# Down projection of a hybrid encoder step: the last token group ends bank by bank, and the first rows' operands are split before the up projection's last sums

## Chip, cores and metric

The kernel runs on one core of a Trainium2 chip. The metric is device time in microseconds (us) of one execution; below, times without a unit are us. Before the change, three runs took 1442.82, 1444.15 and 1447.29; the median is 1444.15.

## The reference

One inference step of a one-layer encoder over 1024 prompt tokens and 32 sample tokens of width 1024: a mixer of three kinds of heads, then a convolutional feed-forward block. Only the latter matters here:

```python
def conv_ffn(xn, buf, w_up, conv_w, conv_b, w_down):
    up = xn @ w_up
    up, buf = causal_dwconv(up, buf, conv_w, conv_b)
    gate, val = jnp.split(up, 2, axis=-1)
    return (jax.nn.gelu(gate, approximate=True) * val) @ w_down, buf
...
h, ffn_buf = conv_ffn(rms_norm(x, g_ffn_pre[l]), ...)
x = x + rms_norm(h, g_ffn_post[l])
```

`w_up` is 1024 x 5632 and `w_down` 2816 x 1024, all float32. The convolution runs over the last three tokens. The inner width of 2816 makes 22 rows of 128 channels, called rows 0 to 21 here.

## The kernel before

**Precision.** A float32 product is made of three matmuls. `split` (line 104) makes a high part by a cast on ScalarE (line 106) and a low part by a subtraction on VectorE (line 109); `mm3` (lines 99 to 102) adds high x high, high x low and low x high in one PSUM bank. So each operand needs a cast and a subtraction before TensorE can use all of it.

**Up projection.** `up_all` (line 1208) goes over the 22 rows; each is done in two blocks of columns (274 and 256), and each block by seven half-size products instead of eight (Strassen-like). `up_block` (line 1150) copies some of the sums out of PSUM on ScalarE (`keep`, line 1159) and adds them on VectorE (line 1164). Its last step, the product p7 with its copy and two sums, is held back and run inside the next block; the very last one stands behind the loop as `next(late, None)`. `up_finish` (line 1190) then moves the tokens' borders on GpSimd, does the convolution of the row's gate and value (one activation on ScalarE and two multiply-adds on VectorE each), the gelu and the product, and stores the h row to DRAM (`h_d`, line 1206).

**Down projection.** `down_all` (line 1239) covers the tokens in three groups of tiles of 128 tokens: tiles 0, 1 and the 32 sample tokens; tiles 2, 3, 4; tiles 5, 6, 7. In each group it goes over all 22 rows again. `load_h` (line 1267) loads the group's columns of an h row into a staging tile `hr` (two buffers), splits it into `hh` and `hl` (two buffers each), loads 128 x 1024 weights into a raw tile (two buffers, shared with the up projection's weights) and splits each half of these with `weight_halves` (line 1117; tag `op`, seven buffers, each of one half's high and low part).

The first group makes the result transposed: eight banks, each of 128 output channels by 288 tokens, 24 matmuls a row. The other two groups make it upright: for each of three token tiles two banks of 512 output channels, 18 matmuls a row. All 22 rows are added in these six banks, so that they are all done only with row 21.

`finish` (line 1248) ends a token tile: squares with a running sum on ScalarE (line 1256), a product with the gain on VectorE (line 1258), three tiny operations on GpSimd for the root of the mean (lines 1260, 218 and 219), and for each half one multiply-add with the residual on VectorE (line 1264) and one store (line 1265). Its statistics tile `fss` has two buffers. The residuals are loaded four rows before the end (`residual`, line 1242).

**What sets the order.** The instructions are written in program order, and a planner, which runs a simulation of the engines' times, orders each engine's queue from it: what is written earlier has the higher priority, and something written later may be drawn forward when its inputs and a free buffer are there and the engine is idle in the simulation. The resulting order on each engine is fixed. All loads and stores are issued from one queue, SyncE's (SPq).

Of the kernel before, what the change touches and what calls it, by code (L numbers as in the profile page):

```python
# [8 lines left out]
F32 = mybir.dt.float32  # L9
F32R = mybir.dt.float32r  # L10
# [9 lines left out]
DEC = 32  # L20
NTOK = SEQ + DEC
DFF = 2816
NF = DFF // 128
# [12 lines left out]
DGROUPS = [(0, 1, 8), (2, 3, 4), (5, 6, 7)]  # L36


def fcol(u):

    return 128 * u if u < 4 else SMP if u == 8 else GAP_P + 2 + 128 * (u - 4)
# [5 lines left out]
            p6=("S2", "T2"), p7=("S3", "T3"))  # L47
# [43 lines left out]
def body(ctx: ExitStack, tc: tile.TileContext, a: dict):  # L91
    nc = tc.nc
    act, dve, pool, pe, sp = nc.scalar, nc.vector, nc.gpsimd, nc.tensor, nc.sync
# [5 lines left out]
    def mm3(ps, lh, rh, first, last, **kw):  # L99
        pe.matmul(ps, lh[0], rh[0], start=first, stop=False, **kw)  # L100
        pe.matmul(ps, lh[0], rh[1], start=False, stop=False, **kw)  # L101
        return pe.matmul(ps, lh[1], rh[0], start=False, stop=last, **kw)  # L102

    def split(hi, lo, src, eng=None, heng=None):
        if heng is None:
            act.copy(hi, src)  # L106
        else:
            heng.tensor_copy(hi, src)
        (eng or pool).tensor_tensor(lo, src, hi.bitcast(F32), op=ALU.subtract)  # L109
# [1004 lines left out]
            res.append(r)  # L1114
        return res

    def weight_halves(name, src):
        t = praw[1].tile([128, 2, 512], F32R, tag="op", name=name, bufs=7)
        split(t[:, 0], t[:, 1], src, dve)
        return t[:, 0], t[:, 1]  # L1120

# [83 lines left out]
        dve.tensor_tensor(ys[0], ys[0], ys[1], op=ALU.mult)  # L1205
        sp.dma_start(h_d[f], ys[0])

    def up_all(pw_, W0, X, uus, py):

        raw, W = {}, {0: W0}  # L1210
        late = None
        for f in range(NF):
            uu = uus[f % len(uus)]
            if f + 1 < NF:
                raw[f + 1] = up_raw(f + 1)
            for s in range(2):
                if s == 1 and f + 1 < NF:
                    ops = up_operands(f + 1, raw.pop(f + 1))
                    W[f + 1] = next(ops)
                    for _ in ops:  # L1220
                        pass
                blk = up_block(pw_, f, s, W[f], X[s], uu)
                next(blk)
                if late:
                    next(late, None)
                    if s == 0:
                        up_finish(py(), f - 1, uus[(f - 1) % len(uus)])
                        W.pop(f - 1)
                next(blk)
                yield  # L1230
                next(blk)
                late = blk
                yield
        next(late, None)
        up_finish(py(), NF - 1, uus[(NF - 1) % len(uus)])

    praw = []

    def down_all(ph, p6, gp):
        xres = {}  # L1240

        def residual(u):
            n = 128 if u < 8 else DEC
            x = p6.tile([128, 1024], F32, tag="xres", name=f"fr{u}", bufs=4)
            sp.dma_start(x[:n], x2_d[128 * u:128 * u + n, :])
            xres[u] = x

        def finish(u, n, src):

            x = xres.pop(u)  # L1250
            ss = p6.tile([128, 4], F32, tag="fss", name=f"gss{u}", bufs=2)
            jk = p6.tile([128, 1024], BF16, tag="fjk", name=f"gjk{u}", bufs=2)
            ys = []
            for hf in range(2):
                c = slice(512 * hf, 512 * hf + 512)
                act.activation(jk[:n, c], src[hf], AF.Square, accum_out=ss[:n, 2 + hf:3 + hf])
                y = p6.tile([128, 512], F32, tag="yt", name=f"yt{u}{hf}", bufs=4)
                dve.tensor_tensor(y[:n], src[hf], gp[:n, c], op=ALU.mult)
                ys.append(y)
            pool.tensor_tensor(ss[:n, 0:1], ss[:n, 2:3], ss[:n, 3:4], op=ALU.add)  # L1260
            rstd_of(ss[:n, 1:2], ss[:n, 0:1], n, 1, 1024)
            for hf in range(2):
                c = slice(512 * hf, 512 * hf + 512)
                dve.scalar_tensor_tensor(x[:n, c], ys[hf][:n], ss[:n, 1:2], x[:n, c], op0=ALU.mult, op1=ALU.add)
                sp.dma_start(a["yp"][128 * u:128 * u + n, c] if u < 8 else a["ys"][:, c], x[:n, c])

        def load_h(g, f, spans, w):
            r = ph.tile([128, 384], F32, tag="hr", name=f"hr{g}_{f}", bufs=2)
            for (c0, c1, o) in spans:
                sp.dma_start(r[:, o:o + c1 - c0], h_d[f, :, c0:c1])  # L1270
            hh = ph.tile([128, 384], F32R, tag="hh", name=f"hh{g}_{f}", bufs=2)
            hl = ph.tile([128, 384], F32R, tag="hl", name=f"hl{g}_{f}", bufs=2)
            split(hh[:, :w], hl[:, :w], r[:, :w], dve)
            wr = praw[0].tile([128, 1024], F32, tag="raw", name=f"wd{g}_{f}r", bufs=2)
            sp.dma_start(wr, a["w_dn"][f])
            return hh, hl, [weight_halves(f"wd{g}_{f}{hf}", wr[:, 512 * hf:512 * hf + 512]) for hf in range(2)]

        def spans_of(us):
            spans, off, w = [], {}, 0
            for u in us:  # L1280
                n = 128 if u < 8 else DEC
                off[u] = w
                if spans and spans[-1][1] == fcol(u):
                    spans[-1][1] += n
                else:
                    spans.append([fcol(u), fcol(u) + n, w])
                w += n
            return spans, off, w

        def banks_of(g, m):  # L1290

            where = [(psf, "xw", 4)] * 4 + [(psb, "big", 3)] * 3 + [(psf, "sx", 1)]
            return [p.tile([128, 512], F32, tag=t, name=f"pd{g}_{i}", bufs=b) for i, (p, t, b) in enumerate(where[:m])]


        us = DGROUPS[0]
        spans, off, w = spans_of(us)
        banks = banks_of(0, 8)
        for f in range(NF):
            hh, hl, wd = load_h(0, f, spans, w)  # L1300
            if f == NF - 4:
                for u in us:
                    residual(u)
            for d in range(8):
                c = slice(128 * (d % 4), 128 * (d % 4) + 128)
                mm3(banks[d][:, :w], [t[:, c] for t in wd[d // 4]], (hh[:, :w], hl[:, :w]), f == 0, f == NF - 1)
        acc = p6.tile([128, 8, 288], F32, name="accd")
        for d in range(8):
            (act.copy if d % 2 else dve.tensor_copy)(acc[:, d, :], banks[d][:, :w])

        def turned(u):
            n = 128 if u < 8 else DEC
            src = []
            for hf in range(2):
                p, t, b = ((psb, "big", 3), (psf, "sx", 1))[hf]
                ps = p.tile([128, 512], F32, tag=t, name=f"pt{u}{hf}", bufs=b)
                for d in range(4):
                    pe.transpose(ps[:n, 128 * d:128 * d + 128], acc[:, 4 * hf + d, off[u]:off[u] + n], ident)
                src.append(ps[:n])
            finish(u, n, src)  # L1320

        todo = [lambda u=u: turned(u) for u in us]
        for g, us2 in enumerate(DGROUPS[1:], 1):
            spans, off2, w = spans_of(us2)
            banks = banks_of(g, 2 * len(us2))
            for f in range(NF):
                hh, hl, wd = load_h(g, f, spans, w)
                if f == NF - 4:
                    for u in us2:
                        residual(u)  # L1330
                for i, u in enumerate(us2):
                    c = slice(off2[u], off2[u] + 128)
                    for hf in range(2):
                        mm3(banks[2 * i + hf], (hh[:, c], hl[:, c]), wd[hf], f == 0, f == NF - 1)
                if f % 2 == 0 and todo:
                    todo.pop(0)()
            for i, u in enumerate(us2):
                finish(u, 128, banks[2 * i:2 * i + 2])


# [102 lines left out]
    px1 = p8s.enter_context(tc.tile_pool(name="px1", bufs=1, side="right"))  # L1443
    py = []
    X.append(None)
    for i, _ in enumerate(up_all(pw_, W0, X, uus, lambda: py[0])):
        if i < 2:

            with tc.issue_after(done[0].ins):
                next(last[i])  # L1450
        if i == 1:
            X[1] = col_operands(px1, {f"B{k + 1}{j + 1}": x1[:, 4 * k:4 * k + 4, j, :] for k in range(2) for j in range(2)}, 1)
            p6s.close()
            p5s.close()
            py.append(p9s.enter_context(tc.tile_pool(name="p9", bufs=1, side="left")))
# [3 lines left out]
    sp.dma_start(gp, a["grows"][1:2, :].broadcast_to([128, 1024]))  # L1459
    sp.dma_start(a["p_fc"], fhalo)  # L1460
    sp.dma_start(a["q_fc"], fcache)
    down_all(py[0], p10, gp)
    p9s.close()
    p8s.close()
    p7s.close()
# [130 lines left out]
```

## Time and profile before

| what | value |
| --- | --- |
| median of three runs | 1444.15 us |
| the profiled execution | 1444.85 us |
| its span | 1443.1 us |
| TensorE matmuls busy (PE) | 1378.0 us, 95% |
| TensorE weight loads (PEld) | 1261.5 us, 87% |
| VectorE (DVE) | 1015.6 us, 70% |
| ScalarE (ACT) | 707.0 us, 49% |
| GpSimd (POOL) | 275.8 us, 19% |
| mean granted TensorE clock | 0.979 |

All times in the rows are counted from the start of the span. A row of the timeline gives the start, the time taken, the engine, the line of the kernel, the operation, the tile written, the tiles read, their sizes and the count of instructions merged in it; in brackets stands how long the engine was idle just before, and which instruction ended that. Matmuls overlap in the pipeline, so the distance between two starts, not the time of one, is the rate. The clock is the share of its full rate that TensorE was granted. In this profile the up projection's last products end around 1171 us, the first group of the down projection runs to about 1245, the second to about 1338 and the third to about 1434.

### The profile page before, as it was taken

The numbers are of one execution on the slowest core, as the hardware profiler recorded it, in microseconds if no ns is written. First come the engines' busy times: TensorE is split into PE (matmuls) and PEld (weight loads), VectorE is DVE, ScalarE is ACT, GpSimd is POOL, SyncE is SP. The second block draws the span as 40 slices with busy tenths as digits, with TensorE's granted clock in tenths as the row PEclk, the third lists the DMA queues.
The fourth block names the chain that finished last, engine by engine and source line by source line (L and its number), as shares of the span: only waits on it lengthen the run. The fifth ranks groups of instructions, "written<-read, shape, count | busy, mean of one in ns | idle before, by whom it ended". The sixth has DMA issues, their size and how long they took to land.

```text
span 1443.1 us, 29992 instructions
## 1 busy us (share of the span) xinstructions
PE 1378.0 (95%) x11804; PEld 1261.5 (87%) x11804; DVE 1015.6 (70%) x1832; ACT 707.0 (49%) x1379; POOL 275.8 (19%) x456
## 2 busy tenths in 40 slices
PE   7989999999998998999799999999999999999997
PEld 6989889898887986767699999999999999988785
DVE  5796479657596568675898878788878865654644
ACT  5545556445474545333555555455545555543432
POOL 6531121113121224212221111111111110000101
PEclk9999999999999999999899999999999999999999
DMA  9599778766788754343312221222122266664742
GB/s 341 193 319 346 268 245 296 231 224 227 241 267 315 259 167 158 116 161 96 121 49 98 78 89 60 90 75 89 61 89 75 84 204 220 218 217 166 247 168 103
DMA packets 132436, 255.10 MB, mean 177 GB/s; under 512 B 28647, under 2 KB 79367, under 8 KB 132295
## 3 DMA queue, kind: packets, MB, share of 16 engines
q1 hardware_dynamic: 132295, 253.19, 51.6%
q8 instruction: 92, 1.51, 0.4%
q14 instruction: 49, 0.40, 0.1%
HBM read 192.26 MB, written 60.89 MB: 175 GB/s over the span
## 4 chain that ended last, share of the span: by engine, by line
PE 73%; DVE 13%; DMA 4%; ACT 4%; issue 2%; POOL 2%; SPq 1%; DVEq 0%; ACTq 0%; POOLq 0%
PE pd L101 5%; PE pd L100 5%; PE pd L102 5%; PE pux L100 4%; PE pux L101 4%; PE pux L102 4%; PE pv L102 4%; PE pv L100 4%; PE pv L101 4%; PE puw L102 3%; PE puw L101 3%; PE puw L100 3%; PE mi L692 2%; PE zp L100 2%; PE zp L102 2%
## 5 line engine op out<-in xcount | busy, mean ns | idle before, releaser
L1202 DVE SCALAR_TENSOR_TENSOR y<-uu,fconv_sb,y 128x1060 f32<-128x1060 f32 x88 | 116.3, 1322 | 26.5 <-ACT y L1200 25.7
L100 PE MATMUL pd<-wd,hh 128*128 128x512 f32 x264 | 104.8, 397 | 0.4 <-ACT hh L106 0.3
L101 PE MATMUL pd<-wd,hh 128*128 128x512 f32 x264 | 104.3, 395 | 0.0
L102 PE MATMUL pd<-wd,hl 128*128 128x512 f32 x264 | 90.8, 395 | 0.0
L1196 POOL COPY uu<-uu 128x2 f32<-128x2 f32 x44 | 34.3, 779 | 215.2 <-DVE uu L1164 215.1
L1159 ACT COPY c<-pux 128x274 f32<-128x274 f32 (+1 forms) x132 | 49.1, 375 | 42.0 <-PE pux L102 38.9
L1200 ACT ACTIVATE y<-uu,fconv_sb 128x1060 f32<-128x1060 f32 x44 | 56.1, 1275 | 16.0 <-POOL uu L1197 15.7
L100 PE MATMUL zp<-woh,ch 128*128 128x512 f32 (+1 forms) x144 | 58.2, 411 | 4.1 <-DVE cl L1020 3.1
L100 PEld LDWEIGHTS pd<-wd,hh 128*128 128x128 f32 x264 | 49.5, 187 | 13.1 <-ACT hh L106 1.3
L102 PEld LDWEIGHTS pd<-wd,hl 128*128 128x128 f32 x264 | 49.5, 187 | 12.1
L101 PEld LDWEIGHTS pd<-wd,hh 128*128 128x128 f32 x264 | 49.5, 188 | 11.8
L100 PE MATMUL pv<-wt_0h,xh 128*128 128x256 f32 (+2 forms) x195 | 57.3, 294 | 1.7 <-ACT xh L316 1.7
L101 PE MATMUL zp<-wol,ch 128*128 128x512 f32 (+1 forms) x144 | 58.7, 407 | 0.0
L102 PE MATMUL zp<-woh,cl 128*128 128x512 f32 (+1 forms) x144 | 57.8, 405 | 0.2 <-DVE cl L1020 0.2
L102 PE MATMUL pv<-wt_1h,xl 128*128 128x256 f32 (+2 forms) x195 | 57.2, 293 | 0.5 <-DVE xl L317 0.5
L102 PE MATMUL pv<-wt_0h,xl 128*128 128x256 f32 (+2 forms) x195 | 56.5, 290 | 0.6 <-DVE xl L317 0.6
L101 PE MATMUL pv<-wt_1l,xh 128*128 128x256 f32 (+2 forms) x195 | 56.7, 291 | 0.0
L100 PE MATMUL pv<-wt_1h,xh 128*128 128x256 f32 (+2 forms) x195 | 56.6, 290 | 0.0
L101 PE MATMUL pv<-wt_0l,xh 128*128 128x256 f32 (+2 forms) x195 | 56.2, 288 | 0.1
L218 POOL TENSOR_SCALAR hrs<-hss 128x5 f32<-128x5 f32 (+3 forms) x27 | 14.5, 537 | 196.4 <-DVE hss L888 195.8
L101 PE MATMUL pd<-hl,wd 128*128 128x288 f32 x176 | 51.2, 302 | 0.6 <-DVE hl L109 0.6
L102 PE MATMUL pd<-hh,wd 128*128 128x288 f32 x176 | 51.1, 303 | 0.0
(1663 smaller groups left out, 5171.1 us busy)
## 6 DMA issues: line engine op xcount, KB each, us to landing
h_d<-y SPq DMA_DIRECT2D x22, 530.0 KB, 2.7
wt_0r<-in_w_tok SPq DMA_DIRECT2D x21, 512.0 KB, 5.6
wt_1r<-in_w_tok SPq DMA_DIRECT2D x21, 512.0 KB, 5.9
wt_0l<-lt_d SPq DMA_DIRECT2D x14, 512.0 KB, 4.0
wt_1l<-lt_d SPq DMA_DIRECT2D x14, 512.0 KB, 5.2
qkb<-qkb_d SPq DMA_DIRECT2D x8, 768.0 KB, 6.1
hr<-h_d SPq DMA_DIRECT2D x44, 128.0 KB, 3.1
hr<-h_d SPq DMA_DIRECT2D x22, 192.0 KB, 3.3
```

Source lines behind the costliest of these rows:

```text
L100: pe.matmul(ps, lh[0], rh[0], start=first, stop=False, **kw)
L101: pe.matmul(ps, lh[0], rh[1], start=False, stop=False, **kw)
L102: return pe.matmul(ps, lh[1], rh[0], start=False, stop=last, **kw)
L218: pool.tensor_scalar(out, ss, 1.0 / width, EPS, op0=ALU.mult, op1=ALU.add)
L692: fn(*args, **kw)
L1159: act.copy(t, ps)
L1196: pool.tensor_copy(u[:, GAP_P:GAP_P + 2], u[:, GAP_S - 2:GAP_S])
L1200: act.activation(y, u, AF.Identity, scale=fconv[:, j, 2:3], bias=fconv[:, j, 3:4])
L1202: dve.scalar_tensor_tensor(y, uu[i][:, s:s + NCOL], fconv[:, j, s:s + 1], y, op0=ALU.mult, op1=ALU.add)
```

## The change

There are three edits.

First, `load_h` and `spans_of` move out of `down_all`, and `up_all` gets a function `ahead` that it calls just before the held-back last product. `ahead` loads and splits rows 0 and 1 of the first group; `down_all` finds them in `begun`.

Second, buffers: `hh` and `hl` get four each, `fss` four; four more operand tiles (tag `opd`) are taken from the pool of the down projection's own tiles for the weights of the last two rows of the last group.

Third, in the last group the products of its last four rows (18 to 21) are not made row by row. They are kept, and after row 21 is loaded, each token tile and each half takes its four rows at once, 12 matmuls into one bank; `finish` of a tile stands right behind its second half.

```diff
-    def weight_halves(name, src):
-        t = praw[1].tile([128, 2, 512], F32R, tag="op", name=name, bufs=7)
+    def weight_halves(name, src, deep=None):
+        if deep:
+            t = deep.tile([128, 2, 512], F32R, tag="opd", name=name, bufs=4)
+        else:
+            t = praw[1].tile([128, 2, 512], F32R, tag="op", name=name, bufs=7)
...
+        ahead()
         next(late, None)
         up_finish(py(), NF - 1, uus[(NF - 1) % len(uus)])
...
+    def load_h(ph, g, f, spans, w, deep=None):
...
-            hh = ph.tile([128, 384], F32R, tag="hh", name=f"hh{g}_{f}", bufs=2)
-            hl = ph.tile([128, 384], F32R, tag="hl", name=f"hl{g}_{f}", bufs=2)
+        hh = ph.tile([128, 384], F32R, tag="hh", name=f"hh{g}_{f}", bufs=4)
+        hl = ph.tile([128, 384], F32R, tag="hl", name=f"hl{g}_{f}", bufs=4)
...
-            ss = p6.tile([128, 4], F32, tag="fss", name=f"gss{u}", bufs=2)
+            ss = p6.tile([128, 4], F32, tag="fss", name=f"gss{u}", bufs=4)
...
-            hh, hl, wd = load_h(0, f, spans, w)
+            hh, hl, wd = begun.pop(f, None) or load_h(ph, 0, f, spans, w)
...
+            n_end = 4 if g == len(DGROUPS) - 1 else 0
+            end = []
+
+            def products(i, u, hf, f, hh, hl, wd):
+                c = slice(off2[u], off2[u] + 128)
+                mm3(banks[2 * i + hf], (hh[:, c], hl[:, c]), wd[hf], f == 0, f == NF - 1)
+
             for f in range(NF):
-                hh, hl, wd = load_h(g, f, spans, w)
+                ops = load_h(ph, g, f, spans, w, p6 if f >= NF - n_end // 2 else None)
...
+                if f >= NF - n_end:
+                    end.append((f, *ops))
+                    continue
...
             for i, u in enumerate(us2):
+                for hf in range(2):
+                    for ops in end:
+                        products(i, u, hf, *ops)
                 finish(u, 128, banks[2 * i:2 * i + 2])
...
+    begun = {}
+
+    def ahead():
+        spans, _, w = spans_of(DGROUPS[0])
+        for f in range(2):
+            begun[f] = load_h(py[0], 0, f, spans, w)
```

More of the change, by code (lines that the diff above doesn't have):

```diff
@@ L1206, in up_finish, with up_all @@
         sp.dma_start(h_d[f], ys[0])
-    def up_all(pw_, W0, X, uus, py):
+    def up_all(pw_, W0, X, uus, py, ahead):
         raw, W = {}, {0: W0}
@@ L1237, in body, with spans_of, down_all @@
     praw = []
-    def down_all(ph, p6, gp):
+    def load_h(ph, g, f, spans, w, deep=None):
+        r = ph.tile([128, 384], F32, tag="hr", name=f"hr{g}_{f}", bufs=2)
+        for (c0, c1, o) in spans:
+            sp.dma_start(r[:, o:o + c1 - c0], h_d[f, :, c0:c1])
+        hh = ph.tile([128, 384], F32R, tag="hh", name=f"hh{g}_{f}", bufs=4)
+        hl = ph.tile([128, 384], F32R, tag="hl", name=f"hl{g}_{f}", bufs=4)
+        split(hh[:, :w], hl[:, :w], r[:, :w], dve)
+        wr = praw[0].tile([128, 1024], F32, tag="raw", name=f"wd{g}_{f}r", bufs=2)
+        sp.dma_start(wr, a["w_dn"][f])
+        return hh, hl, [weight_halves(f"wd{g}_{f}{hf}", wr[:, 512 * hf:512 * hf + 512], deep) for hf in range(2)]
+    def spans_of(us):
+        spans, off, w = [], {}, 0
+        for u in us:
+            n = 128 if u < 8 else DEC
+            off[u] = w
+            if spans and spans[-1][1] == fcol(u):
+                spans[-1][1] += n
+            else:
+                spans.append([fcol(u), fcol(u) + n, w])
+            w += n
+        return spans, off, w
+    def down_all(ph, p6, gp, begun):
         xres = {}
@@ L1265, in finish @@
                 sp.dma_start(a["yp"][128 * u:128 * u + n, c] if u < 8 else a["ys"][:, c], x[:n, c])
[L1267 to L1270, printed above, removed]
-            hh = ph.tile([128, 384], F32R, tag="hh", name=f"hh{g}_{f}", bufs=2)
-            hl = ph.tile([128, 384], F32R, tag="hl", name=f"hl{g}_{f}", bufs=2)
[L1273 to L1288, printed above, removed]
         def banks_of(g, m):
@@ L1330, in down_all @@
                         residual(u)
+                if f >= NF - n_end:
+                    end.append((f, *ops))
+                    continue
                 for i, u in enumerate(us2):
-                    c = slice(off2[u], off2[u] + 128)
                     for hf in range(2):
-                        mm3(banks[2 * i + hf], (hh[:, c], hl[:, c]), wd[hf], f == 0, f == NF - 1)
+                        products(i, u, hf, f, *ops)
                 if f % 2 == 0 and todo:
@@ L1445, in body @@
     X.append(None)
-    for i, _ in enumerate(up_all(pw_, W0, X, uus, lambda: py[0])):
+    begun = {}
[3 more added lines that the diff above has]
+            begun[f] = load_h(py[0], 0, f, spans, w)
+    for i, _ in enumerate(up_all(pw_, W0, X, uus, lambda: py[0], ahead)):
         if i < 2:
@@ L1461, in body @@
     sp.dma_start(a["q_fc"], fcache)
-    down_all(py[0], p10, gp)
+    down_all(py[0], p10, gp, begun)
     p9s.close()
```

## The prediction

> **What bounds the kernel now.** I read the page first, then the table of windows over the feed-forward half, then the timelines of TensorE, ScalarE, VectorE and the DMA queue where that table shows a hole, and last the timeline of the final 12 us.
>
> ```profile
> PE 1378.0 (95%) x11804; PEld 1261.5 (87%) x11804; DVE 1015.6 (70%) x1832; ACT 707.0 (49%) x1379; POOL 275.8 (19%) x456
> ```
>
> TensorE sets the time. A change that moves none of its work can only win where it stands idle or runs at a low clock. The windows (length; busy time and instructions of PE, PEld, DVE, ACT, POOL; granted clock; DMA share; GB/s) show where that is:
>
> ```profile
> 1172.00:1176.00 4.00, 3.92 (x30) 3.69 (x28) 2.62 (x4) 1.82 (x3) 2.12 (x4) 1.00 0.86 235
> 1176.00:1180.00 4.00, 1.51 (x9) 1.25 (x9) 3.96 (x6) 2.70 (x6) 0.00 (x0) 0.88 1.00 352
> 1180.00:1184.00 4.00, 4.00 (x17) 4.00 (x18) 2.62 (x5) 1.14 (x2) 0.00 (x0) 0.50 1.01 316
> 1184.00:1188.00 4.00, 4.00 (x26) 4.00 (x25) 1.52 (x4) 1.53 (x3) 0.00 (x0) 0.76 0.92 304
> ...
> 1382.00:1431.00 49.00, 49.00 (x212) 39.35 (x211) 17.58 (x30) 15.57 (x30) 0.00 (x0) 1.00 0.37 132
> 1431.00:1443.00 12.00, 3.06 (x14) 2.12 (x12) 7.65 (x12) 3.69 (x12) 3.85 (x9) 0.81 0.34 131
> ```
>
> Two holes touch this change: 1176 to 1188, where the down projection takes over from the up projection (idle, then a clock of 0.50), and the last 9 us behind the last matmul. First the hole at the hand-over, on TensorE:
>
> ```profile
> 1175.63 0.29 PE L102 MATMUL pd<-hh,wd 128*128 128x288 f32 x1
> 1177.89 1.36 PE L100 MATMUL pd<-hh,wd 128*128 128x288 f32 x8 [1.97 <-ACT hh L106]
> 1179.85 0.61 PE L101 MATMUL pd<-hl,wd 128*128 128x288 f32 x1 [0.60 <-DVE hl L109]
> ...
> 1183.86 2.12 PE L100 MATMUL pd<-hh,wd 128*128 128x288 f32 x8
> ...
> 1187.97 1.23 PE L100 MATMUL pd<-hh,wd 128*128 128x288 f32 x8
> ...
> 1191.17 1.23 PE L100 MATMUL pd<-hh,wd 128*128 128x288 f32 x8
> ```
>
> A row of the first group is 24 matmuls, eight of them on line 100, so each "x8" opens a row. 1187.97 to 1191.17 is an undisturbed row: 3.20 us, 0.133 a matmul. Rows 0 and 1 ran between and behind the last products of the up projection; 1177.89 is row 2, 1183.86 row 3, 1187.97 row 4. Without a hole row 2 would start at 1175.63 + 0.13 = 1175.76 and row 4 at 1182.16. Row 4 comes 5.81 later. The gaps are 2.13 (1175.76 to 1177.89) and 0.89 (1177.89 + 8 x 0.133 = 1178.96 to 1179.85), together 3.02; the other 2.79 is the low clock behind them.
>
> Both gaps are waits for the split of the h row: hh (ScalarE) and hl (VectorE).
>
> ```profile
> 756.50 0.43 ACT L106 CAST hh<-hr 128x288 fp32r<-128x288 f32 x1 [2.35 <-DMA hr<-h_d]
> ...
> 1168.15 0.62 ACT L106 CAST wd<-wd_2r 128x512 fp32r<-128x512 f32 x1 [0.28 <-PE puw L102]
> ...
> 1174.23 1.27 ACT L1200 ACTIVATE y<-uu,fconv_sb 128x1060 f32<-128x1060 f32 x1 [2.18 <-POOL uu L1197]
> ...
> 1176.39 0.60 ACT L106 CAST wd<-wd_3r 128x512 fp32r<-128x512 f32 x1
> ...
> 1177.42 0.43 ACT L106 CAST hh<-hr 128x288 fp32r<-128x288 f32 x1
> ...
> 1186.90 1.14 ACT L106 CAST wd<-wd_6r 128x512 fp32r<-128x512 f32 x2 [2.31 <-DMA wd_6r<-in_w_dn]
> ```
>
> The planner had the first h row split at 756.50, over 400 us early, as soon as it existed. Row 2's split comes at 1177.42, behind the last sums' activations, though its weights were cast at 1168.15. The reason is in the code: hh and hl have two buffers each, held by rows 0 and 1 until TensorE is through with them. The h rows themselves were not late, as the DMA queue shows:
>
> ```profile
> 811.04 0.80 SPq L1270 DMA_DIRECT2D hr<-h_d  x2
> ...
> 1181.60 0.33 SPq L1275 DMA_DIRECT2D wd_6r<-in_w_dn  x1
> ```
>
> The issue at 811.04 is row 3's, waiting in its staging buffer for the rest of the up projection.
>
> **The change, part by part.** *Rows 0 and 1 ahead of the last product.* Moved past the last up-projection pieces are 4 weight casts, 2 h casts, 6 subtractions, 4 hr and 2 weight DMAs; passed on ScalarE are one c copy, two y and one gelu, on VectorE two sums, four y steps and the product, on POOL the halo copies, on SP the last h store. By the rows above the planner did nearly all of that already: row 2's weights were split before the last sums. Zero, then; a bound from above is in the slower rival.
>
> *hh and hl from two to four buffers.* Rows 2 and 3 are then split around 800 to 850 us like rows 0 and 1, and their four pieces leave the crowded stretch after 1176. What is late next? I put each row where an unbroken TensorE would want it and look when its weights are there in this trace:
>
> ```profile
> 1168.84 0.69 DVE L109 TENSOR_TENSOR wd<-wd_2r,wd 128x512 fp32r<-128x512 f32 x1
> ...
> 1178.14 0.69 DVE L109 TENSOR_TENSOR wd<-wd_3r,wd 128x512 fp32r<-128x512 f32 x1
> ...
> 1187.55 1.29 DVE L109 TENSOR_TENSOR wd<-wd_6r,wd 128x512 fp32r<-128x512 f32 x2 [2.48 <-ACT wd L106]
> ```
>
> Row 2 (wanted 1175.76) is there at 1169.53. Row 3's second half (wanted half a row after 1178.96, at 1180.56) is there at 1178.83. Row 6 (wanted 1175.76 + 4 x 3.20 = 1188.56) has its first half at 1187.55 + 0.65 = 1188.20: 0.36 to spare, because its load, issued at 1181.60, lands only at 1186.90 while the DMA share is 1.0. So the chain just closes, and I count the whole 5.81, with 0 and 5.81 as bounds. Cover gone, it costs the same again.
>
> *The other place where two buffers pinch*, early in the last group, where hr stood in the DMA queue behind an output's residual load:
>
> ```profile
> 1356.33 1.56 PE L102 MATMUL pd<-wd,hl 128*128 128x512 f32 x6
> 1358.20 0.50 PE L100 MATMUL pd<-wd,hh 128*128 128x512 f32 x1 [0.31 <-ACT hh L106]
> ```
>
> Six matmuls from 1356.33 end their turn at 1356.33 + 6 x 0.233 = 1357.73 (0.233 is 4.20 over 18, below), so 0.47 is lost and should go.
>
> *The end.* Rows 18 to 21 of the last group are now multiplied bank by bank, 12 matmuls (2.8 us) into each of six banks, so tiles 5 and 6 are finished while TensorE still works; four statistics buffers instead of two let the third tile start at once. TensorE's sum is unchanged. Before:
>
> ```profile
> 1431.10 0.86 PE L102 MATMUL pd<-wd,hl 128*128 128x512 f32 x3
> 1431.59 0.60 ACT L1256 ACTIVATE gjk<-pd 128x512 bf16<-128x512 f32 x1 [5.62 <-PE pd L102]
> 1432.18 0.59 ACT L1256 ACTIVATE gjk<-pd 128x512 bf16<-128x512 f32 x1
> 1433.67 0.40 PE L102 MATMUL pd<-wd,hl 128*128 128x512 f32 x1
> 1434.12 1.40 DVE L1264 SCALAR_TENSOR_TENSOR fr<-yt,gss,fr 128x512 f32<-128x512 f32 x2
> 1435.64 0.60 ACT L1256 ACTIVATE gjk<-pd 128x512 bf16<-128x512 f32 x1 [1.62 <-DVE fr L1264]
> 1436.22 0.59 ACT L1256 ACTIVATE gjk<-pd 128x512 bf16<-128x512 f32 x1
> 1438.56 1.41 DVE L1264 SCALAR_TENSOR_TENSOR fr<-yt,gss,fr 128x512 f32<-128x512 f32 x2
> ```
>
> From the start of a bank's last matmul to its square takes 0.49 (1431.10 to 1431.59). So the last square can start at 1433.67 + 0.49 = 1434.16 instead of 1436.22: 2.06. From there to the last multiply-add took 2.34 in the last tile and 1.94 (1432.18 to 1434.12) in the first, so 2.06 to 2.46; I take 2.2, the middle. Stores and the close behind it stay.
>
> What it adds: operands of row 21 are wanted 6 to 10 us sooner, and its h split waits for row 17's buffer. Rows come every 4.20 now:
>
> ```profile
> 1412.40 0.62 ACT L106 CAST wd<-wd_19r 128x512 fp32r<-128x512 f32 x1 [2.64 <-PE pd L102]
> ...
> 1416.60 0.62 ACT L106 CAST wd<-wd_20r 128x512 fp32r<-128x512 f32 x1 [2.64 <-PE pd L102]
> ```
>
> The end phase starts four rows before 1433.90, at T = 1417.10, and wants row 21 after nine matmuls, at 1419.2. Row 19's second half is cast at 1412.40 and its raw buffer free by about 1413.8; row 21's load goes then. With wd_6r's slow 5.3 us it lands at 1419.1, its first half is split 1.3 later: 1.2 late. Rows 20 and 21 no longer wait for a buffer of the seven (four of their own), so row 20 is early. Queued behind row 21's cast on ScalarE are only the squares of tile 5, wanted at T + 2.8. But the DMA share is 0.37 here (window 1382 to 1431), not 1.0, so I take no stall: 0, bounds 0 and 1.2.
>
> *Sum.* 5.81 + 0.47 + 2.2 = 8.48. The profiled execution took 1444.85 (span 1443.1 and 1.75 around it), so 1436.4; the median of the runs shown, 1444.15, is 0.7 lower, so 1435.7. For the thin 0.36 at row 6 I give back 0.3: **1436.0**.
>
> **The rivals.** *(a) The stall only moves.* The planner keeps rows 2 and 3 late, or row 6 takes the hole over: a landing 2.5 us later than in this trace makes a gap of over 2 us, and the clock falls again. For it: 0.36 to spare and a DMA share of 1.0. Against it: with h rows 4 and 5 fetched long before, there is less to fetch there. The 5.81 goes: 1444.15 - 2.67 = 1441.5. Chance 0.15.
>
> *(b) The low clock stays.* If it does not come from the gap, only the gaps are won: 1444.15 - 3.02 - 0.47 - 2.2 = 1438.5. For the gap as its cause speaks the only other stretch of the feed-forward half with a low clock, also behind idle time:
>
> ```profile
> 700.00:710.00 10.00, 4.28 (x18) 3.52 (x16) 8.53 (x10) 5.23 (x12) 4.89 (x6) 0.73 0.38 120
> 710.00:720.00 10.00, 7.28 (x38) 6.88 (x39) 5.79 (x9) 4.11 (x7) 0.87 (x4) 0.59 0.66 203
> ```
>
> The Trainium skill ("TensorE: Matmul & The Clock Gate", "What's actually happening") has the clock halve after an idle window of about 3.4 us. By that rule two gaps of 2.13 and 0.89 with 1.07 of work between would not do it, and this rival is what it gives; the trace has 0.50 behind just these gaps, and I follow the trace. Chance 0.07.
>
> *(c) Slower: the six casts take ScalarE's turn.* Set ahead in priority, 4 x 0.62 + 2 x 0.43 = 3.34 stand before the copies that the last product waits for. TensorE idles past about 2 us, the clock falls there (2.79), the chain to row 3 slips as much, and the old hole stays. 1444.15 + 3.34 + 2.79 - 2.67 = 1447.6. It decides only if those casts aren't done earlier; in this trace they are. Chance 0.03.
>
> **How the numbers follow.** The forecast has 0.75. Its own range is 1433.5 (the larger 2.46 without the 0.3 given back, 1435.4; less the 1.3 that the lowest run lies under the median, and half of that again for the kernel after) to 1438.0 (a third of the 5.81 kept by a short gap). For 8 in 10 it reaches up to rival (a): 1433.5 to 1441.5. A measurement here tells about 0.3%, 4.3 us: faster means under 1439.8. Forecast and (b) and a part of (a), where the gap returns without the clock, lie there: 0.78. Same: the rest of (a) and a little, 0.18. Slower: (c), 0.04.
>
> **What would show it.** Right: hh and hl casts of rows 2 and 3 near 800 us, no wait of TensorE for hh at the hand-over, windows from 1176 to 1188 at 1.00 with busy 4.00; tile 5's square about 14 us before the last matmul ends; four stores gone before the last two; about 7 us instead of 9 behind the last matmul. Wrong: a PE wait on wd or a DMA near row 6, a clock under 1.00 without a gap, or a wait for wd_21r within the last 17 us.

## The result and the profile after

| | before | after |
|---|---|---|
| median of 6 runs each | 1444.43 us (1442.82 to 1449.55) | 1435.9 us (1433.15 to 1439.9) |
| after / before | | 0.9947, 95% interval 0.9931 to 0.9963 |
| profiled execution | 1444.85 us, span 1443.1 | 1436.23 us, span 1434.5 |

Faster by 8.5 us between the medians, 0.59%; the ratio of the runs, with its interval, says 0.53%. The forecast was 1436.0. TensorE does the same 11804 matmuls; its busy line on the page after:

```profile
PE 1375.7 (96%) x11804; PEld 1260.3 (88%) x11804; DVE 1013.2 (71%) x1832; ACT 705.5 (49%) x1379; POOL 274.1 (19%) x456
```

To see where the time came from I cut both traces at the same three instructions: the start of the up projection's last matmul, the first matmul of the second group (the first 128x512 one on these lines), and the last matmul. The rows of before (TensorE's timeline; the last matmul, 1433.67, stands in the prediction):

```profile
1170.85 0.28 PE L102 MATMUL pux<-T3h,S_21h 128*128 128x256 f32 x1
...
1245.57 0.39 PE L100 MATMUL pd<-wd,hh 128*128 128x512 f32 x1
```

and of after, with two of row 6 between:

```profile
1171.49 0.28 PE L102 MATMUL pux<-T3h,S_21h 128*128 128x256 f32 x1
...
1189.21 0.30 PE L100 MATMUL pd<-hh,wd 128*128 128x288 f32 x1
...
1189.74 0.43 PE L102 MATMUL pd<-hh,wd 128*128 128x288 f32 x2
...
1240.41 0.39 PE L100 MATMUL pd<-wd,hh 128*128 128x512 f32 x1
...
1427.58 0.40 PE L102 MATMUL pd<-wd,hl 128*128 128x512 f32 x1
```

| stretch (us) | before | after | won | predicted |
|---|---|---|---|---|
| hand-over: 1170.85 to 1245.57; 1171.49 to 1240.41 | 74.72 | 68.92 | 5.80 | 5.81 |
| groups two and three: to the last matmul | 188.10 | 187.17 | 0.93 | 0.47 |
| tail: last matmul to the span's end | 9.43 | 6.92 | 2.51 | 2.2 |

Together 9.24. The last up-projection matmul came 0.64 later in this execution, so the span is shorter by 8.60. Where no hole is left these lengths repeat to some hundredths from kernel to kernel, while the whole times of one kernel spread over several us, so the experiments below are read by them first.

The windows that answer to those of before (same columns):

```profile
1172.00:1176.00 4.00, 4.00 (x32) 4.00 (x31) 3.03 (x5) 1.59 (x3) 2.12 (x4) 1.00 0.91 226
1176.00:1180.00 4.00, 4.00 (x32) 4.00 (x31) 3.55 (x5) 3.58 (x7) 0.00 (x0) 1.00 1.03 341
1180.00:1184.00 4.00, 4.00 (x32) 4.00 (x31) 2.82 (x5) 0.00 (x0) 0.00 (x0) 1.00 1.02 348
1184.00:1188.00 4.00, 4.00 (x32) 4.00 (x31) 1.66 (x3) 1.57 (x4) 0.00 (x0) 1.00 0.93 282
...
1348.00:1360.00 12.00, 12.00 (x53) 9.64 (x52) 6.70 (x12) 5.28 (x10) 0.00 (x0) 1.00 0.83 286
1426.00:1434.50 8.50, 1.98 (x9) 1.26 (x7) 2.79 (x4) 0.69 (x2) 0.94 (x3) 0.87 0.32 121
```

Where before had 1.51 of 4.00 busy and then a clock of 0.50, TensorE is busy throughout at 1.00. The DMA share there is as high as before (0.91 to 1.03): the transfers did not get easier, only the wait for the split tiles is gone. ScalarE's timeline of after shows why, and how the end runs:

```profile
793.27 0.43 ACT L106 CAST hh<-hr 128x288 fp32r<-128x288 f32 x1 [0.22 <-DMA hr<-h_d]
...
814.04 0.43 ACT L106 CAST hh<-hr 128x288 fp32r<-128x288 f32 x1 [0.30 <-DMA hr<-h_d]
...
1410.81 1.14 ACT L106 CAST wd<-wd_21r 128x512 fp32r<-128x512 f32 x2 [2.42 <-DMA wd_21r<-in_w_dn]
...
1418.04 0.60 ACT L1283 ACTIVATE gjk<-pd 128x512 bf16<-128x512 f32 x1 [5.67 <-PE pd L102]
...
1428.02 0.60 ACT L1283 ACTIVATE gjk<-pd 128x512 bf16<-128x512 f32 x1 [2.02 <-PE pd L102]
```

The casts at 793.27 and 814.04 are those of rows 2 and 3, nearly 400 us ahead of their use; before, only rows 0 and 1 were split early. The last square starts 0.44 behind the start of the last matmul. On VectorE:

```profile
1188.55 1.29 DVE L109 TENSOR_TENSOR wd<-wd_6r,wd 128x512 fp32r<-128x512 f32 x2 [1.80 <-ACT wd L106]
...
1424.32 1.41 DVE L1291 SCALAR_TENSOR_TENSOR fr<-yt,gss,fr 128x512 f32<-128x512 f32 x2 [0.50 <-POOL gss L219]
...
1429.92 1.41 DVE L1291 SCALAR_TENSOR_TENSOR fr<-yt,gss,fr 128x512 f32<-128x512 f32 x2 [0.50 <-POOL gss L219]
```

Tile 6's outputs are done at 1425.73, ahead of the last matmul, so only two of the six stores are left behind it.

### The profile page after: what moved, and what is told of

Its sections match the earlier page's. It is cut to its first block, busy times and chain, and to the rows that moved or that the text cites. A ratio compares the mean times of both kernels' runs of the same rounds, so it can differ in the third digit from the quotient of the medians.

```text
span 1434.5 us, 30024 instructions
## 1 busy us (share of the span) xinstructions
PE 1375.7 (96%) x11804; PEld 1260.3 (88%) x11804; DVE 1013.2 (71%) x1832; ACT 705.5 (49%) x1379; POOL 274.1 (19%) x456
## 3 DMA queue, kind: packets, MB, share of 16 engines
q8 instruction: 92, 1.51, 0.4%
## 4 chain that ended last, share of the span: by engine, by line
PE 79%; DVE 10%; DMA 4%; ACT 3%; issue 1%; POOL 1%; SPq 0%; DVEq 0%; POOLq 0%; ACTq 0%
PE pd L100 6%; PE pd L101 6%; PE pd L102 6%; PE pux L100 4%; PE pux L101 4%; PE pux L102 4%; PE pv L100 4%; PE pv L102 4%; PE pv L101 4%; PE puw L102 3%; PE puw L101 3%; PE puw L100 3%; PE pf L100 2%; PE pf L102 2%; PE pf L101 2%; PE mi L692 2%
## 5 line engine op out<-in xcount | busy, mean ns | idle before, releaser
L102 PE MATMUL pd<-wd,hl 128*128 128x512 f32 x264 | 104.0, 395 | 0.0
```

## The experiments

My theory after the result: two buffers of hh and hl made the hand-over hole and both small holes of the last group; the new end makes the tail; the early call of rows 0 and 1 does nothing. Its rivals: the early call closes the hole; the low clock has another cause than the idle time. Each kernel is before or after with one edit. The profiled lengths of all of them:

| kernel | hand-over | groups 2 and 3 | tail | ratio to before (95%) |
|---|---|---|---|---|
| before | 74.72 | 188.10 | 9.43 | |
| after | 68.92 | 187.17 | 6.92 | 0.9947 (0.9931 to 0.9963) |
| before, four buffers of hh, hl | 68.92 | 187.18 | 8.89 | 0.9962 (0.9954 to 0.9971) |
| before, new end only | 73.75 | 187.13 | 6.87 | 0.9987 (0.9976 to 0.9998) |
| before, early call only | 73.25 | 188.57 | 9.40 | 0.9992 (0.9979 to 1.0005) |
| after without the early call | 68.92 | 187.19 | 6.85 | 0.9944 (0.9932 to 0.9956) |
| before, 24 filler matmuls | 72.87 | 188.47 | 9.37 | 0.9995 (0.9980 to 1.0010) |
| before, 8 filler matmuls | 72.68 | 188.48 | 9.43 | 0.9988 (0.9975 to 1.0001) |
| before, three buffers | 69.34 | 187.20 | 8.86 | 0.9950 (0.9933 to 0.9967) |
| before, four statistics buffers only | 74.75 | 187.57 | 9.49 | 0.9990 (0.9971 to 1.0008) |

**Four buffers alone.**

```
-            hh = ph.tile([128, 384], F32R, tag="hh", name=f"hh{g}_{f}", bufs=2)
-            hl = ph.tile([128, 384], F32R, tag="hl", name=f"hl{g}_{f}", bufs=2)
+            hh = ph.tile([128, 384], F32R, tag="hh", name=f"hh{g}_{f}", bufs=4)
+            hl = ph.tile([128, 384], F32R, tag="hl", name=f"hl{g}_{f}", bufs=4)
```

> The kernel before with hh and hl at four buffers and nothing else. My theory: the hand-over stall is a matter of these buffers alone, so no wait of TensorE for hh or hl there, the clock stays at 1.00 from 1176 to 1188, and the first 512-wide matmul of the second group starts 5.8 us sooner relative to the up projection's last product; with the small holes of the last group 6.3 to 6.7 us in all, ratio 0.9955. The rival that splitting rows 0 and 1 ahead is what closes the hole: no gain here, ratio 1.000, the waits for hh of 2.0 us and for hl of 0.6 us still there.

The hand-over is 68.92, that of after to the hundredth, without the early call. The holes of the last group go too (187.18), and, not expected, 0.54 of the tail. Why the tail: before, row 21's split had to wait for a buffer (the cast for products of line 101, the low part for the cast), as its rows on ScalarE

```profile
1425.46 0.51 ACT L106 CAST hh<-hr 128x384 fp32r<-128x384 f32 x1 [3.63 <-PE pd L101]
```

and VectorE show:

```profile
1426.01 0.56 DVE L109 TENSOR_TENSOR hl<-hr,hh 128x384 fp32r<-128x384 f32 x1 [3.40 <-ACT hh L106]
```

The planner put row 21's products with hl behind the others (the three in one group at 1431.10 in the prediction), and the first square could start only at 1431.59, 2.08 ahead of the last matmul's start. That it did so for the late split is argued: in the trace the low part was there at 1426.57, before row 21 began, and the times that the planner reckoned with are not known. With four buffers the first square starts here, on ScalarE, against a last matmul at 1427.91, 3.01 ahead:

```profile
1424.90 0.60 ACT L1256 ACTIVATE gjk<-pd 128x512 bf16<-128x512 f32 x1 [9.24 <-PE pd L102]
```

VectorE, which waits for the first square and, as the statistics buffers show below, sets the old tail, begins 0.93 sooner by the last matmul as well (1425.62 here, 1432.31 before). It loses 0.40 of that in short waits, and about 0.53 remain.

**Three buffers.** The same two lines with bufs=3.

> The kernel before with three buffers for hh and hl. My theory: row 2 is split far ahead, row 3 only when row 0 is through, and its split then queues on ScalarE behind the last sums' activations and is there about 1 us after row 3 could start. So a gap under 1.2 us, no fall of the clock, and a stretch from the last product to the second group between 68.9 and 70.2 us; ratio about 0.9965. Rival: two rows more are needed, and the stretch stays at 73 us or over.

One buffer more is nearly enough: row 2 no longer waits, the wait that I expected at row 3 did not come, and the clock stays at 1.00. Most of the 0.42 that remain stands in row 7, on TensorE (three matmuls from 1188.98 end their turn at 1189.38; 0.26 of wait follow, and 0.10 of a slow restart, 0.23 to the next matmul instead of 0.133)

```profile
1188.98 0.56 PE L100 MATMUL pd<-hh,wd 128*128 128x288 f32 x3
1189.64 0.40 PE L101 MATMUL pd<-hl,wd 128*128 128x288 f32 x1
1189.87 0.30 PE L102 MATMUL pd<-hh,wd 128*128 128x288 f32 x1
```

where its hl, queued on VectorE behind the low parts of a late weight row, ends at 1189.58:

```profile
1187.92 1.29 DVE L109 TENSOR_TENSOR wd<-wd_7r,wd 128x512 fp32r<-128x512 f32 x2 [1.45 <-ACT wd L106]
1189.13 0.45 DVE L109 TENSOR_TENSOR hl<-hr,hh 128x288 fp32r<-128x288 f32 x1
```

The fourth buffer keeps that subtraction out of the crowded stretch.

**The early call alone, and all but the early call.** The first is before with load_h moved out and called for rows 0 and 1 ahead of the last sums, hh and hl at two buffers, two statistics buffers and no end phase (n_end = 0); the second is after with one line out:

```
             late = blk
             yield
-        ahead()
         next(late, None)
```

> Only rows 0 and 1 loaded and split ahead of the last product, two buffers, the old end. My theory: nothing, since the planner had drawn these splits forward already: ratio 1.000, the waits for hh and hl at the hand-over as before. The rival of the prediction (six casts take ScalarE's turn) would give 3 to 6 us more, ratio 1.002 to 1.004; the rival that this part closes the hole gives 0.996.

> The kernel after without the part that splits rows 0 and 1 ahead. My theory: the time of the kernel after, ratio to before 0.9945 within 0.001. The rival that this part matters: between 0.996 and 0.9985, with a wait of TensorE at the hand-over.

Alone the call leaves the hole; taken out of the change it leaves 68.92, 187.19 and 6.85. Its worth is nothing that could be measured, in either place. After without it is the simplest of the fast versions, 1434.35 at the median of its runs against 1443.71 of before beside it; no run here was clearly faster than after. The hole with the call alone, on TensorE:

```profile
1181.39 1.56 PE L100 MATMUL pd<-hh,wd 128*128 128x288 f32 x8 [2.14 <-ACT hh L106]
1183.35 0.61 PE L101 MATMUL pd<-hl,wd 128*128 128x288 f32 x1 [0.39 <-DVE hl L109]
```

It waits for the same tile, hh, and about as long as before (2.14 of idle time, before 1.97). That its hand-over is 73.25 and not 74.72 is the clock, below, and nothing that the call does: the same came with the new end alone (73.75), which touches nothing there.

**The new end alone.** After with the early call out and two buffers of hh and hl for all rows but the last four of the last group:

```
-        hh = ph.tile([128, 384], F32R, tag="hh", name=f"hh{g}_{f}", bufs=4)
-        hl = ph.tile([128, 384], F32R, tag="hl", name=f"hl{g}_{f}", bufs=4)
+        e = g == 2 and f >= NF - 4
+        hh = ph.tile([128, 384], F32R, tag="hhe" if e else "hh", name=f"hh{g}_{f}", bufs=4 if e else 2)
+        hl = ph.tile([128, 384], F32R, tag="hle" if e else "hl", name=f"hl{g}_{f}", bufs=4 if e else 2)
```

> Only the new end: last four rows of the last group bank by bank, with h tiles of their own (four buffers), four statistics buffers; hh and hl otherwise at two, nothing split ahead. My theory: the hand-over keeps its 5.8 us, and only the stretch from the start of the last matmul to the end of the span shrinks, from 9.43 to 6.9; ratio 0.9983. Rival: part of the 0.93 us that the last two groups gained comes from the end phase too; then the stretch from the second group's first matmul to the last matmul is also under 188.1 us.

The tail is that of after (6.87), 2.56 less than before. Four buffers alone bring 0.54 of that and not on top of it. Both small holes of the last group are gone as well (187.13), though its early rows still have two buffers. My theory had laid those holes on the two buffers alone; that part falls.

**Four statistics buffers alone.**

```
-            ss = p6.tile([128, 4], F32, tag="fss", name=f"gss{u}", bufs=2)
+            ss = p6.tile([128, 4], F32, tag="fss", name=f"gss{u}", bufs=4)
```

> The kernel before with four statistics buffers for the closing of the token tiles, nothing else. My theory: the last tile's square no longer waits for the first tile's multiply-add (1.62 us), so the stretch from the last matmul to the end falls from 9.43 to between 7.8 and 8.9 us; the hand-over stays. Whether the two small holes early in the last group (0.92 us together) go as well is open: the stretch from the second group's first to the last matmul is 187.2 us if these holes hang on the statistics buffers, 188.1 us if on hh and hl.

The tail stays (9.49), where I expected 7.8 to 8.9. The squares do move: the last one starts 0.79 behind the last matmul's start (1432.01 here), before 2.55. But VectorE gains nothing by it. Its twelve operations for the three tiles run without a break from 1430.66 to 1438.31, as they did before from 1432.31 to 1439.97, and only the stores come behind them. ScalarE and VectorE here:

```profile
1432.80 0.62 ACT L1256 ACTIVATE gjk<-pd 128x512 bf16<-128x512 f32 x1
...
1430.66 1.89 DVE L1258 TENSOR_TENSOR yt<-pd,gp 128x512 f32<-128x512 f32 x3 [5.74 <-ACT gjk L1256]
...
1436.24 2.07 DVE L1264 SCALAR_TENSOR_TENSOR fr<-yt,gss,fr 128x512 f32<-128x512 f32 x3
```

and VectorE of before:

```profile
1432.31 1.89 DVE L1258 TENSOR_TENSOR yt<-pd,gp 128x512 f32<-128x512 f32 x3 [5.75 <-ACT gjk L1256]
```

So the old tail is VectorE's work of some 7.65, begun some 1.35 ahead of the last matmul's start in both kernels, and not the wait of a square for a statistics buffer. The new end helps because tiles 5 and 6 are through VectorE before the last matmul. Whether it needs the four statistics buffers at all was not run; in the trace of after, tile 5 is done with its buffer at 1422.41 and tile 7's first square starts only at 1425.30.

Half of the 0.93 goes (187.57): of the two holes of the last group one is left. So these holes hang on the order in which the planner sets hr, residual loads and splits there, which each of three edits shifts, and not on one buffer count. By which chain a statistics buffer reaches the split of an h row stays open. Nor is the size of the two holes fixed: with the early call alone and with the fillers they are in the same place and take 1.28 to 1.38 together (188.47 to 188.57 against 187.19), before 0.92.

**Filler matmuls: is the low clock the idle time's?** Before, with matmuls of a zero operand added to the open sums behind row 1, 24 or 8 of them. They add nothing to the sums and leave the buffers and the loads as they were; one small subtraction on VectorE makes the zeros:

```
+                z = ph.tile([128, 288], F32R, name="zr")
+                dve.tensor_tensor(z, hh[:, :w].bitcast(F32), hh[:, :w].bitcast(F32), op=ALU.subtract)
...
+            if f == 1:
+                for k in range(24):
+                    pe.matmul(banks[k % 8][:, :w], z[:, :128], z, start=False, stop=False)
```

> The kernel before with 24 extra matmuls by a tile of zeros, added into the open banks between rows 1 and 2 of the first group (3.2 us at the full rate, the sums unchanged), in place of the idle time at the hand-over; the h split of row 2 is as late as before. My theory, that the low clock comes from the idle time: the clock stays at 1.00, row 2 runs from about 3.2 us behind row 1's end, and the stretch from the up projection's last product to the second group is 68.9 + 3.2 = 72.1 us instead of 73.3 to 74.7, though TensorE does more. Rival (the low clock has another cause at this place): 0.50 in the records all the same, 74 us or more.

> The same with 8 matmuls by zeros (1.07 us), so that about 2 us of the 3.0 us of idle time stay. If the clock needs an idle stretch of about two us to fall, it stays at 1.00 here and the stretch is about 68.9 + 3.0 = 72 us; if 2 us in two pieces are enough, it falls as before and the stretch is between 73.2 and 74.7 us.

With 24, TensorE's timeline has 19 of them where the hole was, and row 2 behind them at full rate (8 matmuls, 1.07 to the next):

```profile
1174.87 2.66 PE L1312 MATMUL pd<-zr 128*128 128x288 f32 x19
1177.37 1.23 PE L100 MATMUL pd<-hh,wd 128*128 128x288 f32 x8
1178.44 0.30 PE L101 MATMUL pd<-hl,wd 128*128 128x288 f32 x1
...
1184.46 1.33 PE L100 MATMUL pd<-hh,wd 128*128 128x288 f32 x8 [0.53 <-ACT hh L106]
```

The clock is 1.00 in every window from 1164 to 1196. The stretch: 68.92 + 24 x 0.133 + 0.79 (the wait of row 4, 0.69, and 0.10 of restart) = 72.9; measured 72.87. My 72.1 lacked that wait of row 4. So the stretch is 1.85 shorter with 3.2 us of useless work in it: the low clock comes with TensorE's idle time and goes with it. With 8 fillers the waits stay and are only cut shorter:

```profile
1171.88 0.56 PE L1312 MATMUL pd<-zr 128*128 128x288 f32 x3
1172.99 1.33 PE L100 MATMUL pd<-hh,wd 128*128 128x288 f32 x8 [0.55 <-ACT hh L106]
1174.86 0.40 PE L101 MATMUL pd<-hl,wd 128*128 128x288 f32 x1 [0.54 <-DVE hl L109]
```

Gaps of 0.71 (1171.88 + 0.40 to 1172.99) and 0.80 (1172.99 + 1.07 to 1174.86, 0.10 of it the slow restart), and yet the windows of this kernel keep the clock:

```profile
1172.00:1176.00 4.00, 2.91 (x20) 2.45 (x19) 3.96 (x6) 2.31 (x6) 0.00 (x0) 1.00 1.01 344
1176.00:1180.00 4.00, 4.00 (x32) 4.00 (x31) 2.00 (x4) 1.11 (x2) 0.00 (x0) 1.00 1.00 336
1180.00:1184.00 4.00, 3.40 (x26) 3.17 (x25) 1.69 (x4) 1.50 (x4) 0.00 (x0) 1.00 0.91 314
```

The loss against 68.92, 3.76, is then the fillers (1.07), these two gaps, a third of 0.75 at row 4 (1180.30 to 1181.05) and smaller ones with their restarts. My range for a clock that falls, 73.2 to 74.7, is not reached.

## Why the prediction was right

Point by point, in its own steps.

*The hole at the hand-over, 5.81: right, for the reason given.* Measured 5.80, and four buffers alone give the same. Both parts were as taken: the waits are gone with the buffers, and the low clock with the waits, as the fillers show by themselves. Rival (b), the clock that stays low, is out by the same runs.

*Row 6, 0.36 to spare, 0.3 given back: it held.* Row 6 starts at 1189.21; its first low half is there at 1188.55 + 0.65 = 1189.20, and the planner had set the first product that needs it at 1189.74. So 0.5 to spare, no wait, nothing to give back. Rival (a) stayed away, though not by much: with three buffers row 7 does stop.

*Rows 0 and 1 ahead, zero: right*, shown from both sides. Rival (c) needed casts that the early call puts ahead of the copies; alone or in the change, it does not slow anything.

*The other place where two buffers pinch, 0.47: the term that was mis-sized.* It measured 0.93. I had one hole (1356.33 to 1358.20); there was a second 7 us earlier on TensorE of before, and the step left out that each restart costs something:

```profile
1348.76 0.40 PE L102 MATMUL pd<-wd,hl 128*128 128x512 f32 x1
1349.23 0.50 PE L100 MATMUL pd<-wd,hh 128*128 128x512 f32 x1
1349.56 0.39 PE L101 MATMUL pd<-wd,hh 128*128 128x512 f32 x1
```

From 1348.76 to 1349.23 is 0.47 instead of 0.233, and the first matmul behind a gap takes 0.33 to the next instead of 0.233. So 0.24 + 0.10 here and 0.47 + 0.11 at the other: 0.92. The cause that the step named is only partly right: four or three buffers alone close both holes, but so does the new end alone, with two buffers in these rows, and the statistics buffers alone close one. The second hole has no releaser in its row and is missing from a list of waits; a list of starts that come later than the rate allows would have shown it.

*The end, 2.06 to 2.46, took 2.2: low by 0.3, and the reason for it half wrong.* That tiles 5 and 6 are finished while TensorE works is what pays. That the last tile waited for a statistics buffer, and would start at once with four, was the wrong wait: four alone move its squares and leave the tail at 9.49, since VectorE's operations set it. The sum held all the same, because it took the path of the last tile by itself, and in after that is the path. The last square starts 0.44 behind the last matmul's start (0.49 taken), and from there to the last multiply-add it is 1429.92 - 1428.02 = 1.90, where before's last tile took 2.34 and the first 1.94. So the short figure holds once nothing competes, and the gain, 2.51, lies at the upper end of the range and not in its middle. What lies behind the last multiply-add is 4.58, before 4.54, as assumed.

*Row 21, 1.2 late by one row, taken as no stall: no stall, but the order gave way.* Its cast is at 1410.81, where the phase's first matmuls run (72 x 0.233 = 16.8 ahead of 1427.8). The planner put row 21's products of the first two banks behind rows 18 and 19 of the third. So tile 5's first square is at 1418.04, about 10 us ahead of the end and not the 14 that I named as a sign. That it reckoned with the load is argued; in the trace row 21's last low part was there at 1413.22, about when the prediction's order would have wanted it. It cost nothing, since only the last bank sets the end.

In the sum the two small terms were low by 0.46 and 0.31 and 0.3 was given back for nothing; the profiled execution was 8.62 shorter, against 8.48 and 8.18 with the 0.3. A later start of the stretch (0.64) hid part of that, so that the median came within 0.1 of the forecast is in part luck.

## What to carry over

A wait for a tile that was split early is often a wait for its buffer: compare when the raw data came with when it was converted, and count the buffers before moving calls about. A wait that a row names need not be on the path: the square's wait of 1.62 for a multiply-add could be removed without a gain, since VectorE was busy to the end. A hole on TensorE cost its length, 0.1 for the restart and, at 2 us, an estimated 1.7 to 2.8 more in clock, so a table of clock by window belongs beside the list of waits. Of a change in three parts the largest may be one number: four buffers gave 6 of the 8.5 us, the phase at the end nearly all of the rest, and the early call, the longest part of the diff to follow, nothing.

## What the runs showed of the hardware

*The same hole costs a different amount each time.* Four kernels keep it, with a first gap of about 2 us, and their hand-overs are 74.72, 74.75, 73.75 and 73.25. The difference is how long the clock stays low. With the new end alone, on TensorE and in the windows:

```profile
1177.00 1.67 PE L100 MATMUL pd<-hh,wd 128*128 128x288 f32 x8 [1.98 <-ACT hh L106]
1178.95 0.61 PE L101 MATMUL pd<-hl,wd 128*128 128x288 f32 x1 [0.28 <-DVE hl L109]
```

```profile
1176.00:1180.00 4.00, 2.72 (x12) 2.38 (x13) 4.00 (x6) 1.80 (x5) 0.00 (x0) 0.72 1.00 313
1180.00:1184.00 4.00, 4.00 (x28) 4.00 (x27) 2.08 (x5) 1.14 (x2) 0.00 (x0) 0.85 0.93 289
1184.00:1188.00 4.00, 3.71 (x28) 3.48 (x27) 0.71 (x2) 0.76 (x2) 0.00 (x0) 1.00 0.88 274
```

With the statistics buffers alone:

```profile
1176.74 1.33 PE L100 MATMUL pd<-hh,wd 128*128 128x288 f32 x8 [1.97 <-ACT hh L106]
1178.69 0.61 PE L101 MATMUL pd<-hl,wd 128*128 128x288 f32 x1 [0.63 <-DVE hl L109]
```

```profile
1176.00:1180.00 4.00, 2.63 (x13) 2.40 (x14) 4.00 (x6) 1.54 (x4) 0.00 (x0) 0.75 1.00 319
1180.00:1184.00 4.00, 4.00 (x19) 4.00 (x18) 2.29 (x5) 1.57 (x3) 0.00 (x0) 0.50 0.89 290
1184.00:1188.00 4.00, 4.00 (x29) 4.00 (x28) 1.91 (x4) 2.01 (x4) 0.00 (x0) 0.90 0.73 265
```

In the first the eight matmuls already take 1.67 instead of 1.33, so the clock fell among them, behind a single gap of 2 us. Time at half rate, as an estimate from the granted clock, (1.00 - clock) x 4 us x 2 summed over the windows: 2.24 + 1.20 = 3.4 us; in the second kernel 2.00 + 4.00 + 0.80 = 6.8 us, twice that. Before had the long one (0.96 + 4.00 + 1.92 = 6.9 from the prediction's windows), the early call alone the short one. The clock records in the traces, of which the windows are means, have these lengths as 3.41 and 6.83, and there every stretch at one clock that begins and ends inside a trace is a whole number of 3.41 (in before, 460.80 at full rate up to this fall is 135 of them). Cutting TensorE's idle time (the figures in brackets) by these borders shows what went with the two lengths:

| kernel | 3.41 us at full rate | idle in it | the next 3.41 us | idle in it | then |
|---|---|---|---|---|---|
| before | 1175.65 to 1179.06 | 1.97 | clock 0.50 | 0.60 | 0.50 once more |
| statistics buffers only | 1174.56 to 1177.97 | 1.97 | clock 0.50 | 0.63 | 0.50 once more |
| new end only | 1174.37 to 1177.79 | 1.98 | clock 0.50 | 0.28 | 1.00 |
| early call only | 1178.90 to 1182.31 | 2.14 | clock 0.50 | 0.39 | 1.00 |
| 8 filler matmuls | 1171.73 to 1175.15 | 1.09 | clock 1.00 | 0.00 | 1.00 |

Where the clock fell among the eight matmuls, they ran slower and the second wait was shorter. These are bounds for this place alone: elsewhere (four buffers, 528.0 to 531.4) the clock fell behind 3.27 of 3.40 us busy, with matmuls as small as 32x32, so the idle time of the records is not the whole measure. Between the 73.75 and the 73.25 most of the difference is another wait for hh, at row 4, that only the new end alone has.

The Trainium skill ("TensorE: Matmul & The Clock Gate", "What's actually happening") tells of a free-running window of about 3.4 us, after whole ones of which the clock is changed; one and two such lengths agree with that. Its condition, an idle window of 3.4 us, does not: here one gap of 2 us was enough, while gaps of 0.71 and 0.80 were not. Where between these the bound lies was not tried.

*So the gain differs from execution to execution.* Two lengths are worth some 1.0 to 1.5 us more than one (74.7 against 73.75 and 73.25). That would explain why four buffers alone took 5.9 off the median where the two profiled lengths differ by 7.3 (5.80 + 0.92 + 0.54), as before's hole is shorter in some executions than in the profiled one; it is argued, not shown, since the timed runs have no traces.
